# Decode softmax in three visits, values from three groups sooner, conv loads by pairs, and the last additions on one engine

## The chip, the core and the metric

The kernel runs on one core of a Trainium2 chip. The metric is device time in microseconds (us) of one execution; the kernel before is given by the median of three runs. The engines are named as in the profile: PE (TensorE, the matrix engine; PEld its weight loads), DVE (VectorE), ACT (ScalarE), POOL (GpSimd) and SP (SyncE, which here only issues DMAs). Each engine works through its own instructions in order, and semaphores join them.

## What is computed

One layer of a decoder for 512 prompt rows behind 16 learned ones, and 32 rows of eight samples that decode four tokens each over 512 cached positions in pages of 128. With `h` the normalised rows:

```python
q, k, v, ga, cb, cc, ch, gc, ma, mc = split(h @ w_in)        # w_in 2048 x 12288
a = stick_breaking(q, k, v) * silu(ga)                       # 8 heads of 128
c = cb * causal_conv3(cc * ch) * silu(gc)
m = sigmoid(ma + b_ga) * (a @ w_pa) + sigmoid(mc + b_gc) * (c @ w_pc)
y = x + rmsnorm(m @ w_out)

# stick_breaking, in log space:
z = q @ k.T / sqrt(128) + b_h
keep = where(s < t, log_sigmoid(-z), 0)
A = where(s < t, exp(log_sigmoid(z) + sum of keep between s and t), 0)
out = A @ v
```

The samples use the same layer over the cached keys and values in pages that a table names.

## The kernel before, in words

All products stand for fp32 by splitting both sides into a high and a low part (`whi`, `wlo` for weights, `_hi`, `_lo` for rows) and adding three products. So each weight block of 1024x128 is loaded (`raw`, on SP's queue), cast on ACT (`whi`) and subtracted on DVE (`wlo`); five `raw` and three split blocks are kept. The rows lie transposed, features on partitions, 272 queries to a matmul.

The stages, in the time of the profile: the start and the norm, to 60; heads 0 to 3 with their attention, and keys and values of heads 4 to 7 (these go to DRAM), to 390; the gate `ga` and the conv inputs, and then the two sigmoid gates (820 to 1191.8). The last ones are Strassen-Winograd products (`seven`): of two column blocks each, seven products of 24 matmuls instead of eight, with the sums `h11 - h12` and so on prepared in six tiles `t_hi`, `t_lo` of the pool `tt`. Products 3, 5 and 7 read the first, second and third pair of these tiles, the others read `h_hi`, `h_lo`. From 1191.8 to about 1345 come the conv output products with `w_pc`, 16 column blocks of 48 matmuls, and among them the attention of heads 4 to 7 (`head_here`, which reads keys, values and queries back from DRAM); then the products with `w_pa`, then `w_out` by `seven` again with the way back to rows (`rows`), and a tail that scales each row and adds it to `x` (`finish`).

The decoding of the samples runs beside all of this as a generator, `decode_steps`, which a caller advances by `dec_step(n)`. Its steps are: 64 steps of logits (cached keys `kpage` on DVE times queries, `pr`, then summed on ACT into `junk` with an accumulator, or on DVE); then the softmax in two visits, over 1024 columns at once; then the values: cached pages `vpage` on POOL's queue, eight buffers, 80 matmuls of 32x512 each in one of four column strips of PE (`tile_position`), 64 with cached pages and 16 with the new rows (`v_new`), and a copy `ob` and four transposes behind each twenty. `dec_group` is called behind each of 32 gate groups and says how many steps are taken there:

```python
        if n <= 29:
            dec_step(1 if 4 < n <= 20 else 1 + n % 2, "logits")
        elif n == 30:
            dec_step(64, "weights")
        else:
            dec_step(1)
```

Between the gates and the conv products, eight blocks of `c_scr` are loaded into tiles of the pool `g3` (four buffers, made once `tt` is closed), and split into `c_hl`, which takes the place of `h_hi` (tag "A").

The order of the instructions on each engine is fixed when the kernel is built, by a scheduler that places every instruction by its own estimate of times; `keep_in_program_order` (`pin` in the new lines) holds an instruction among its neighbours on its engine. ACT needs a table of functions for each kind: Exp, Ln, Sigmoid; where a function isn't in the loaded one, a load (ACT_TABLE_LOAD) stands in front of it.

Of the kernel before, what the change touches and what calls it, by code (L numbers as in the profile page):

```python
# [59 lines left out]
def hybrid_step_kernel(  # L60
# [341 lines left out]
    def softplus_parts(e, l, r, t, src, bias, neg_bias=None):  # L402

        act.activation(e, src, AF.Abs, bias=bias)
        act.activation(e, e, AF.Exp, scale=-1.0)
        act.activation(l, e, AF.Ln, bias=one_c[:e.shape[0]])
        act.activation(r, src, AF.Relu, bias=bias)
# [114 lines left out]
    def attend(pl, h, khi, klo, vhi, vlo, qr):  # L522
# [18 lines left out]
        def tl(name, g, dt=F32):  # L541
            return pl.tile([P, GW[g]], dt, name=name + str(GW[g]), bufs=1 if g == "A" else 2)
# [62 lines left out]
    def head_now(h):  # L605
# [4 lines left out]
        dec_step(1, "part")  # L610
# [25 lines left out]
    def decode_steps():  # L636
# [50 lines left out]
        with tc.tile_pool(name="dec2", bufs=1, side="right") as d2:  # L687
# [9 lines left out]
            tc.keep_in_program_order(act.preload_act_table_set(LNEXP))  # L697
# [3 lines left out]
            softplus_parts(e[:TS, :BHT], l[:TS, :BHT], rn, t[:TS, :BHT], zn, zero_c[:TS])  # L701
            softplus_parts(e, l, r, t, zf, zero_c)
            mask_new(rn)
# [7 lines left out]
            for pg in reversed(range(NPG)):  # L711
                rp = r[:, pg * BHT:(pg + 1) * BHT]
                pz = z_ps()[:, :BHT]
                pe.matmul(pz, lhsT=neg_u.bitcast(F32), rhs=rp, start=True, stop=False)
                pe.matmul(pz, lhsT=neg_one.bitcast(F32), rhs=S, start=False, stop=True)
                dve.tensor_add(flat(z_all[:, pg]), pz, flat(z_all[:, pg]))
                act.activation(flat(A_all[:, pg]), flat(z_all[:, pg]), AF.Exp)
                if pg > 0:
                    dve.tensor_add(S, S, rp)
# [78 lines left out]
    ttp = tctx.enter_context(tc.tile_pool(name="tt", bufs=1))  # L798
# [468 lines left out]
```

## Time and profile before

| | us |
|---|---|
| median of 3 runs | 1667.27 |
| lowest and highest run | 1665.84, 1668.06 |
| the profiled execution | 1665.04 |
| its span | 1663.5 |
| PE busy in the span | 1604.2 (96%) |
| DVE, ACT, POOL busy | 1254.3, 997.6, 268.3 |
| mean granted clock of PE | 0.985 |

The profile is of one execution. Its span runs from the first to the last recorded event; 1.5 us of the execution lie around it. Busy time is by the profiler's records, and some matmuls may be missing from them. "PEclk" is the granted clock as a share of the full 2.4 GHz; 0.50 is the lower level, 1.2 GHz. A wait is given with what ended it last. "DMA share" is the mean busy share of the 16 DMA engines, and may pass 1.00 a little.

### The profile page before, as it was taken

The page shows a single profiled execution, that of the slowest core. Times are in us where ns is not written, and L with a number is a line of the kernel's source. Part 1 is how long each engine was busy: PE and PEld are TensorE (multiplying, and loading weights), DVE is VectorE, ACT ScalarE, POOL GpSimd, SP SyncE. Part 2 cuts the span into 40 slices and gives each one's busy share as a digit, 9 for nine tenths or more (in the row PEclk, how much of TensorE's full clock was granted, in tenths as well). Part 3 has the DMA queues.
Part 4 walks back from the last instruction along what each step waited for, and adds up shares of the span by engine and source line. Part 5 has one row for each costly group of instructions (what it writes and reads, how often), then busy time and mean ns, then how long its engine had stood idle before and what let it go on. Part 6 is the DMA issues. An engine that isn't in the chain of part 4 may idle for free.

```text
span 1663.5 us, 31665 instructions
## 1 busy us (share of the span) xinstructions
PE 1604.2 (96%) x12174; PEld 1537.3 (92%) x12174; DVE 1254.3 (75%) x1669; ACT 997.6 (60%) x2549; POOL 268.3 (16%) x476
## 2 busy tenths in 40 slices
PE   7999999999999999999999999999989999999995
PEld 6999999999999999999999999878657999999995
DVE  4538888798879898989888888855346667877775
ACT  6247887746765656565667677953356663445552
POOL 0033233222101010000011011031323230000002
PEclk7999999999999999999999999999989999999998
DMA  9265545435544444444455454364866555533335
GB/s 225 77 177 155 155 144 160 143 119 173 177 129 124 130 139 128 133 123 134 134 167 163 145 173 136 103 206 147 266 228 217 160 161 171 157 108 97 94 105 193
DMA packets 306445, 252.72 MB, mean 152 GB/s; under 512 B 11570, under 2 KB 276854, under 8 KB 305190
## 3 DMA queue, kind: packets, MB, share of 16 engines
q1 hardware_dynamic: 276965, 157.44, 33.0%
q0 software_dynamic: 29296, 93.26, 17.4%
q8 instruction: 95, 1.56, 0.4%
q14 instruction: 57, 0.46, 0.1%
q10 hardware_dynamic: 32, 0.01, 0.0%
HBM read 217.95 MB, written 32.71 MB: 151 GB/s over the span
## 4 chain that ended last, share of the span: by engine, by line
PE 65%; issue 10%; DVE 7%; ACT 7%; DMA 3%; POOL 1%; POOLq 0%; DVEq 0%; SPq 0%; ACTq 0%
PE mm L251 22%; PE mm L845 21%; PE o L845 17%; ACT junk L662 2%; DVE pr L656 2%; ACT whi L235 2%; DMA raw<-in_w_in 2%; DVE wlo L236 1%; PE z L591 1%; PE o L601 1%; PE z L537 1%; PE z L845 1%; PE tp L745 1%; DVE xa L1154 0%; DMA kpage<-in_cache_k 0%
## 5 line engine op out<-in xcount | busy, mean ns | idle before, releaser
L235 ACT CAST whi<-raw 128x1024 fp32r<-128x1024 f32 x251 | 262.8, 1049 | 260.6 <-PE o L845 76.2
L236 DVE TENSOR_TENSOR wlo<-raw,whi 128x1024 fp32r<-128x1024 f32 x251 | 306.4, 1221 | 83.2 <-ACT whi L235 62.9
L845 PE MATMUL mm<-h_hi,whi 128*128 128x272 f32 (+1 forms) x1152 | 334.2, 290 | 4.7 <-ACT whi L235 4.6
L845 PE MATMUL mm<-h_lo,whi 128*128 128x272 f32 (+1 forms) x1152 | 332.5, 289 | 0.0
L845 PE MATMUL mm<-h_hi,wlo 128*128 128x272 f32 (+1 forms) x1152 | 332.2, 290 | 0.0
L845 PE MATMUL o<-t_hi,whi 128*128 128x272 f32 (+1 forms) x864 | 253.3, 293 | 7.2 <-DVE c L871 3.1
L845 PE MATMUL o<-t_hi,wlo 128*128 128x272 f32 (+1 forms) x864 | 250.9, 290 | 1.5 <-DVE wlo L236 1.5
L845 PE MATMUL o<-t_lo,whi 128*128 128x272 f32 (+1 forms) x864 | 250.7, 290 | 0.0
L236 DVE TENSOR_TENSOR wlo<-s,whi 128x1024 fp32r<-128x1024 f32 x126 | 154.6, 1227 | 98.4 <-ACT whi L235 98.2
L845 PEld LDWEIGHTS mm<-h_hi,whi 128*128 128x128 f32 x1152 | 217.4, 189 | 9.4 <-ACT whi L235 6.4
L845 PEld LDWEIGHTS mm<-h_lo,whi 128*128 128x128 f32 x1152 | 217.0, 188 | 2.5 <-issue 2.5
L845 PEld LDWEIGHTS mm<-h_hi,wlo 128*128 128x128 f32 x1152 | 216.4, 189 | 2.8 <-issue 2.5
L662 ACT ACTIVATE junk<-pr 128x128 f32<-128x128 f32 x592 | 182.7, 309 | 29.4 <-DVE pr L656 17.2
L235 ACT CAST whi<-s 128x1024 fp32r<-128x1024 f32 x126 | 131.6, 1045 | 100.2 <-PE o L845 31.1
L251 PE MATMUL mm<-h_hi,whi 128*128 128x280 f32 (+1 forms) x640 | 187.2, 293 | 0.0
L251 PE MATMUL mm<-h_hi,wlo 128*128 128x280 f32 (+1 forms) x640 | 187.0, 293 | 0.0
L251 PE MATMUL mm<-h_lo,whi 128*128 128x280 f32 (+1 forms) x640 | 186.7, 292 | 0.0
L845 PEld LDWEIGHTS o<-t_hi,whi 128*128 128x128 f32 x864 | 164.0, 190 | 16.1 <-issue 5.0
L845 PEld LDWEIGHTS o<-t_hi,wlo 128*128 128x128 f32 x864 | 164.1, 190 | 2.4 <-DVE wlo L236 2.4
L845 PEld LDWEIGHTS o<-t_lo,whi 128*128 128x128 f32 x864 | 164.7, 191 | 0.0
L656 DVE TENSOR_TENSOR pr<-kpage,qb 128x1024 f32<-128x1024 f32 x128 | 152.3, 1218 | 8.1 <-DMA qb<-q_scr 3.7
L251 PEld LDWEIGHTS mm<-h_hi,whi 128*128 128x128 f32 x640 | 120.5, 188 | 0.7
(362 smaller groups left out, 3463.8 us busy)
## 6 DMA issues: line engine op xcount, KB each, us to landing
raw<-in_w_in SPq DMA_DIRECT2D x192, 512.0 KB, 4.3
kpage<-in_cache_k POOLq DMA_DIRECT2D x64, 256.0 KB, 3.4
qb<-q_scr POOLq DMA_DIRECT2D x32, 512.0 KB, 5.7
vpage<-in_cache_v POOLq DMA_DIRECT2D x64, 256.0 KB, 5.4
raw<-in_w_out SPq DMA_DIRECT2D x32, 512.0 KB, 4.1
gate_scr<-g POOLq DMA_DIRECT2D x32, 272.0 KB, 3.4
gt<-gate_scr POOLq DMA_DIRECT2D x16, 544.0 KB, 4.0
raw<-in_w_pc SPq DMA_DIRECT2D x16, 512.0 KB, 4.8
```

The costliest lines, as they stand in the source:

```text
L235: act.copy(hi, x)
L236: dve.tensor_sub(lo, x, hi.bitcast(F32))
L251: pe.matmul(o, lhsT=w, rhs=r[:, t0:t1], start=(k == 0 and n == 0), stop=(k == nk - 1 and n == 2))
L537: pe.matmul(zt[:m, c0:c0 + n], lhsT=l[:, s0:s0 + m], rhs=r[:, ts:ts + n], start=(c0 == 0 and i == 0), stop=(i == 2), skip_group_check=True)
L591: pe.matmul(o, lhsT=l, rhs=x, start=False, stop=(i == len(ops) - 1), skip_group_check=True)
L601: pe.matmul(ot[:, ts - NMETA:ts - NMETA + n], lhsT=l[:m, st, :], rhs=x[:m, c0:c0 + n], start=False, stop=(g == GROUPS[-1] and i == 2), ski ...
L656: dve.tensor_mul(pr, kt.unsqueeze(1).broadcast_to([P, 2, 512]), qt))
L662: act.activation(junk, pr[:, t, h * P:(h + 1) * P], AF.Copy, accum_out=z_all[:, pg, b, 4 * hf + h, 2 * i + t:2 * i + t + 1])
L745: pe.matmul(po[32 * j:32 * (j + 1), :], lhsT=lhs, rhs=rhs, start=(pg == 0), stop=(pg == NPG), tile_position=(0, 32 * j), skip_group_check= ...
L845: pe.matmul(o, lhsT=l[:, k, :], rhs=r, start=(start and k == 0 and m == 0), stop=(stop and k == 7 and m == 2), skip_group_check=True)
```

## The change

It has eight parts:

- heads 0 to 3 advance the decoding by six steps each where they did five;
- `dec_group` takes the logits up to group 28 (seven steps are left to it there), the softmax in groups 28, 29 and 30, and two steps of values in each further group;
- the softmax has three visits: pages 2 and 3 with the new rows, pages 0 and 1, and the last Exp over 1024 columns at once, its ACT instructions pinned;
- the table for Exp and Ln is loaded behind the last gate's sigmoid, and no longer in the middle of the `w_out` products;
- `tt` becomes three pools, `tt0` to `tt2`, and each is given back by itself;
- the eight loads of `c_scr` go by two into four tiles, `head_here` gets its inputs from a pool of its own (`headin`), the first of them loaded ahead, and `gt` moves from POOL's queue to SP's;
- in `rows`, the last 32 rows have a PSUM tile of their own, and their product is laid out as 128x512 (`ogr`), so that one addition does them; a matmul with `to4` brings their factor to the 128 partitions;
- in `finish` all additions are on DVE, most of them 1024 wide, none on POOL, and the stores go out on SP's and ACT's queues in turn.

The core of the diff:

```diff
         khi, klo = k_split(np_, k_proj(h))
-        dec_step(1, "part")
+        dec_step(2, "part")
...
-            pn = z_ps()[:TS, :BHT]
-            pe.matmul(pn, lhsT=neg_u.bitcast(F32)[:TS, :TS], rhs=rn, start=True, stop=True)
-            dve.tensor_add(zn, pn, zn)
-            act.activation(zn, zn, AF.Exp)
+            for p0 in (2, 0):
+                pin(act.preload_act_table_set(LNEXP))
+                if p0:
+                    softplus_parts(e[:TS, :BHT], l[:TS, :BHT], rn, t[:TS, :BHT], zn, zero_c[:TS], pin)
+                    mask_new(rn)
+                c = slice(p0 * BHT, (p0 + 2) * BHT)
+                softplus_parts(e[:, c], l[:, c], r[:, c], t[:, c], zf[:, c], zero_c, pin)
+                if p0:
+                    pn = z_ps()[:TS, :BHT]
+                    pe.matmul(pn, lhsT=neg_u.bitcast(F32)[:TS, :TS], rhs=rn, start=True, stop=True)
+                    dve.tensor_add(zn, pn, zn)
+
+                for pg in (p0 + 1, p0):
+                    rp = r[:, pg * BHT:(pg + 1) * BHT]
+                    pz = z_ps()[:, :BHT]
+                    pe.matmul(pz, lhsT=neg_u.bitcast(F32), rhs=rp, start=True, stop=False)
+                    pe.matmul(pz, lhsT=neg_one.bitcast(F32), rhs=S, start=False, stop=True)
+                    dve.tensor_add(flat(z_all[:, pg]), pz, flat(z_all[:, pg]))
+                    if pg > 0:
+                        dve.tensor_add(S, S, rp)
+                yield
+            pin(act.preload_act_table_set(LNEXP))
+            pin(act.activation(zn, zn, AF.Exp))
             mask_new(zn)
-            yield
...
-        if n <= 29:
+        if n <= 27:
             dec_step(1 if 4 < n <= 20 else 1 + n % 2, "logits")
-        elif n == 30:
-            dec_step(64, "weights")
+        elif n == 28:
+            dec_step(64, "logits")
+            dec_step(1)
+        elif n <= 30:
+            dec_step(1)
         else:
-            dec_step(1)
+            dec_step(2)
...
-    ttp = tctx.enter_context(tc.tile_pool(name="tt", bufs=1))
-    t_hi = [ttp.tile([P, 8, HU], F32R, name=f"t_hi{i}") for i in range(3)]
-    t_lo = [ttp.tile([P, 8, HU], F32R, name=f"t_lo{i}") for i in range(3)]
+    t_hi, t_lo = [], []
+    for i in range(3):
+        ttp = tctx.enter_context(tc.tile_pool(name=f"tt{i}", bufs=1))
+        t_hi.append(ttp.tile([P, 8, HU], F32R, name=f"t_hi{i}"))
+        t_lo.append(ttp.tile([P, 8, HU], F32R, name=f"t_lo{i}"))
     h_f, l_f = h_hi.bitcast(F32), h_lo.bitcast(F32)
...
                 act.activation(gs[m][:, by_query(m, half)], b, AF.Sigmoid, bias=gate_bias(j + m, w))
+            if j + 2 * w == KD:
+                tc.keep_in_program_order(act.preload_act_table_set(LNEXP))
             for m in range(2):
                 gate_out(j + m, w, gs[m])
...
+    hl = cctx.enter_context(tc.tile_pool(name="headin", bufs=1))
     cp = cctx.enter_context(tc.tile_pool(name="later", bufs=1))
-    for k in range(8):
-        cr = g3.tile([P, 2, TQ], F32, tag="gt", name="cr")[:, 0, :]
-        nc.sync.dma_start(cr, c_scr[k])
-        split_evac(c_hl[:, k, :], c_hl[:, 8 + k, :], cr, cr)
+    cp2 = cctx.enter_context(tc.tile_pool(name="later2", bufs=1))
+
+    def head_loads(h):
+        kr = hl.tile([P, T], F32, name="kr")
+        nc.sync.dma_start(kr, k_scr[h])
+        qr = hl.tile([P, PQ], F32, name="qr")
+        nc.sync.dma_start(qr, qt_scr[h][:, 0:PQ])
+        vn = hl.tile([P, 5, P], F32, name="vn")
+        nc.sync.dma_start(vn[:, 0:4, :], vn_scr[h][0:512].rearrange("(a p) d -> p a d", p=P))
+        nc.sync.dma_start(vn[0:16, 4, :], vn_scr[h][512:TP])
+        return kr, vn, qr
+
+    loaded = head_loads(NOW)
+    for k in range(0, 8, 2):
+        cr = g3.tile([P, 2, TQ], F32, tag="gt", name="cr")
+        for i in range(2):
+            nc.sync.dma_start(cr[:, i, :], c_scr[k + i])
+            split_evac(c_hl[:, k + i, :], c_hl[:, 8 + k + i, :], cr[:, i, :], cr[:, i, :])
 
     def gated(h, x, sg):
 
...
+        kr, vn, qr = loaded if h == NOW else head_loads(h)
+        ot = attend(cp, h, *k_split(cp, kr), *v_split(cp, vn), qr, cp2)
         gated(h, ot, sg_load(h)[:, 0, 0:PQ])
...
-        pool.dma_start(gt, gate_scr[j][:, 1, :])
+        nc.sync.dma_start(gt, gate_scr[j][:, 1, :])
...
+                pe.transpose(out=pr, in_=tb[:, ROWS[4][0]:ROWS[4][0] + REST], identity=ident)
             for b, i in enumerate(ii):
                 square(i, j, pt[:, b * P:(b + 1) * P], P)
             dve.tensor_mul(og4[:, ii[0]:ii[-1] + 1, cs], pt[:, :n].rearrange("p (i c) -> p i c", c=P),
                            g.unsqueeze(1).broadcast_to([P, len(ii), P]))
             if rest:
-                square(4, j, pt[:REST, n:n + P], REST)
-                dve.tensor_mul(og_rest(cs), pt[:REST, n:n + P], g[:REST])
-
-        def finish(ii, npool):
+                square(4, j, pr, REST)
+                r0, c0 = j // 4 * REST, j % 4 * P
+                dve.tensor_mul(ogr[r0:r0 + REST, c0:c0 + P], pr, g[:REST])
...
+            queues = cycle((nc.sync, act))
             for b, i in enumerate(ii):
-                n = ROWS[i][1]
+                if i == 4:
+                    continue
+                for c0, c1 in zip(cuts[b], cuts[b][1:]):
+                    xc = xs_[i][:, c0:c1]
+                    dve.scalar_tensor_tensor(out=xc, in0=og4[:, i, c0:c1], scalar=rs[:, b:b + 1], in1=xc,
+                                             op0=ALU.mult, op1=ALU.add)
+                    p0, p1, dst = outs[i][0]
+                    next(queues).dma_start(dst[:, c0:c1], xc[p0:p1])
+                for p0, p1, dst in outs[i][1:]:
+                    next(queues).dma_start(dst, xs_[i][p0:p1])
+            if ii[-1] == 4:
+                r4 = t_ps()[:, 0:1]
+                pe.matmul(r4, lhsT=to4.rearrange("p a b -> p (a b)"), rhs=rs[:REST, w - 1:w], start=True, stop=True)
+                r4s = op.tile([P, 1], F32, name="r4s")
+                act.copy(r4s, r4)
+                dve.scalar_tensor_tensor(out=xs_[4], in0=ogr, scalar=r4s, in1=xs_[4], op0=ALU.mult, op1=ALU.add)
+                dst = outs[4][0][2]
                 for c in range(4):
-                    cs = slice(c * CW, (c + 1) * CW)
-                    og = og4[:n, i, cs] if i < 4 else og_rest(cs)
-                    xc, r = xs_[i][:n, cs], rs[:n, b:b + 1]
-                    if c < 4 - npool[b]:
-                        dve.scalar_tensor_tensor(out=xc, in0=og, scalar=r, in1=xc, op0=ALU.mult, op1=ALU.add)
-                    else:
-                        act.activation(og, og, AF.Copy, scale=r)
-                        pool.tensor_add(xc, xc, og)
-                    for p0, p1, dst in outs[i]:
-                        nc.sync.dma_start(dst[:, cs], xc[p0:p1])
+                    next(queues).dma_start(dst[:, c * CW:(c + 1) * CW], xs_[4][c * REST:(c + 1) * REST])
 
...
             product(o, both[m], m_rhs(1, 1), False, True)
             act.copy(cols[m][:, half(1)], o)
             rows(j + m, (2, 3), cols[m], g[:, m], True)
-        finish((2, 3, 4), (1, 1, 2))
+        finish((2, 3, 4), ((0, D // 2, D), (0, D // 2, 3 * CW, D)))
     mctx.close()
 
```

Three places show how the order moves. First, SP's queue at the passage from the gates to the conv products; `cr` are the tiles for `c_scr`, `kr`, `vn`, `qr` the inputs of head 4. Before:

```order
L229 DMA raw<-in_w_pc 128x8x128 x7
L1008 DMA cr<-c_scr 128x544 x4
L229 DMA raw<-in_w_pc 128x8x128
L1008 DMA cr<-c_scr 128x544 x4
L1023 DMA kr<-k_scr 128x560
L1025 DMA vn<-vn_scr 128x4x128
```

After:

```order
L229 DMA raw<-in_w_pc 128x8x128 x4
L1037 DMA cr<-c_scr 128x544 x8
L229 DMA raw<-in_w_pc 128x8x128
L1025 DMA kr<-k_scr 128x560
L1027 DMA qr<-qt_scr 128x512
L1029 DMA vn<-vn_scr 128x4x128
```

The eight loads of `c_scr` now stand together behind four `w_pc` blocks; they stood in two fours behind seven and eight of them.

Second, PE at the same passage: `o` and `t_hi` are of the last gate product, `tp` with `vpage` or `v_new` are value matmuls, `tp` with `ident` the transposes of their result, `mm` with `c_hl` the conv products. Before:

```order
L845 MATMUL o<-t_hi_5007,wlo 128x272
L745 MATMUL tp<-vpage,z_all 32x512 x3
L745 MATMUL tp<-v_new,z_new 32x512 x4
L753 MATMUL tp<-ident,ob 128x128 x4
L745 MATMUL tp<-vpage,z_all 32x512 x5
L251 MATMUL mm<-c_hl,whi 128x272 x4
L251 MATMUL mm<-c_hl,wlo 128x272
```

After, 60 rows into the conv products:

```order
L251 MATMUL mm<-c_hl,wlo 128x272
L251 MATMUL mm<-c_hl,whi 128x272
L752 MATMUL tp<-vpage,z_all 32x512
L251 MATMUL mm<-c_hl,whi 128x272
L251 MATMUL mm<-c_hl,wlo 128x272
L251 MATMUL mm<-c_hl,whi 128x272 x2
L752 MATMUL tp<-vpage,z_all 32x512
```

Twelve value matmuls stood in a heap before the first conv products, with the transposes of the first twenty among them. Now these transposes have gone ahead into the gates, seven value matmuls are left at the head of the conv products (not shown), and the next ten stand one by one among them.

Third, ACT in the group with the longest stretch between two weight casts (`whi`); `junk` sums logits, `g` is a gate's sigmoid, `de` belongs to the softmax. Before:

```order
L235 CAST whi<-s 128x1024
L662 ACTIVATE junk,z_all<-pr 128x128
L990 ACTIVATE g<-c,bg 128x272
L662 ACTIVATE junk,z_all<-pr 128x128 x7
L990 ACTIVATE g<-o,bg 128x272
L662 ACTIVATE junk,z_all<-pr 128x128 x4
L697 ACT_TABLE_LOAD
L990 ACT_TABLE_LOAD
L990 ACTIVATE g<-c,bg 128x272
L404 ACTIVATE de<-z_new,zero_c 32x256
L859 ACTIVATE o<-mm 128x272
L235 CAST whi<-s 128x1024
```

After:

```order
L664 ACTIVATE junk,z_all<-pr 128x128 x6
L1002 ACTIVATE g<-o,bg 128x272
L723 ACT_TABLE_LOAD
L664 ACTIVATE junk,z_all<-pr 128x128 x3
L871 ACTIVATE o<-mm 128x272
L664 ACTIVATE junk,z_all<-pr 128x128
L1002 ACT_TABLE_LOAD
L1002 ACTIVATE g<-c,bg 128x272
L664 ACTIVATE junk,z_all<-pr 128x128 x2
L703 ACT_TABLE_LOAD
L404 ACTIVATE de<-z_new,zero_c 32x256
L235 CAST whi<-s 128x1024
```

A third table load stands in the stretch where there were two, since a sigmoid comes between the two preloads; the number of `junk` is the same.

## Rows read from the trace of the kernel before

**Rows 1.** The page, busy time, share of span and instructions of PE and others:

```profile
PE 1604.2 (96%) x12174; PEld 1537.3 (92%) x12174; DVE 1254.3 (75%) x1669; ACT 997.6 (60%) x2549; POOL 268.3 (16%) x476
```

**Rows 2.** Windows: length, busy PE, PEld, DVE, ACT, POOL, PEclk, DMA share, GB/s.

```profile
1170.00:1180.00 10.00, 10.00 (x75) 7.54 (x74) 2.81 (x3) 3.54 (x5) 3.24 (x6) 1.00 0.75 225
1191.77:1237.45 45.68, 36.22 (x173) 20.45 (x173) 16.40 (x34) 20.58 (x32) 12.89 (x24) 0.89 0.86 290
1200.00:1210.00 10.00, 6.91 (x39) 4.62 (x40) 2.45 (x4) 2.22 (x5) 1.79 (x4) 1.00 1.06 367
1230.62:1237.45 6.83, 6.21 (x27) 5.82 (x28) 3.88 (x12) 6.75 (x11) 1.08 (x2) 0.50 0.41 141
```

**Rows 3.** PE's waits, 1190 to 1235: waiter, releaser: us, times, longest.

```profile
PE mm L251 <- ACT c_hl L423: 4.2, 3, 2.9
PE tp L753 <- ACT ob L750: 2.3, 2, 1.6
PE z L537 <- ACT qhi L423: 1.6, 1, 1.6
```

**Rows 4.** PE's groups, 1191.80 to 1237.40: records | busy us, mean ns | idle before.

```profile
L251 PE MATMUL mm<-c_hl,whi 128*128 128x272 f32 x64 | 17.2, 350 | 4.9 <-ACT c_hl L423 4.2 <-DVE gt L1048 0.6
L745 PE MATMUL tp<-vpage,z_all 128*32 128x512 f32 x38 | 13.2, 627 | 0.6 <-PE tp L753 0.6
L251 PE MATMUL mm<-c_hl,wlo 128*128 128x272 f32 x31 | 9.7, 329 | 0.0
L745 PE MATMUL tp<-v_new,z_new 32*32 32x512 f32 x16 | 2.1, 600 | 0.0
```

**Rows 5.** SP's issues, 1189 to 1206: start, us, queue, line, what.

```profile
1191.87 2.03 SPq L1008 DMA_DIRECT2D cr<-c_scr  x4
...
1198.96 5.88 SPq L1008 DMA_DIRECT2D cr<-c_scr  x4
```

**Rows 6.** Windows of the decode softmax, columns as above.

```profile
1052.00:1080.00 28.00, 23.88 (x160) 22.57 (x159) 21.27 (x29) 27.60 (x46) 3.86 (x4) 0.88 0.33 96
1059.95:1066.78 6.83, 6.43 (x27) 6.11 (x27) 5.24 (x6) 6.78 (x9) 0.00 (x0) 0.50 0.24 76
```

**Rows 7.** PE's waits, 1000 to 1085.

```profile
PE mm L845 <- ACT whi L235: 3.1, 3, 1.7
PE o L845 <- ACT whi L235: 2.3, 1, 2.3
```

**Rows 8.** ACT's groups, 1220 to 1365: one line's table loads.

```profile
L406 ACT ACT_TABLE_LOAD x8 | 10.3, 1283 | 0.1
```

**Rows 9.** PE in time, 1103.5 to 1106: a single value matmul, and the next.

```profile
1104.10 1.05 PE L745 MATMUL tp<-vpage,z_all 128*32 128x512 f32 x2
1105.08 0.39 PE L845 MATMUL o<-t_hi,whi 128*128 128x272 f32 x1
```

**Rows 10.** PE in time, 1170.8 to 1173.2: five value matmuls, two rounds.

```profile
1171.05 1.91 PE L745 MATMUL tp<-vpage,z_all 128*32 128x512 f32 x12
```

**Rows 11.** A window among heads 0 to 3, columns as above.

```profile
220.00:240.00 20.00, 20.00 (x155) 19.71 (x155) 19.13 (x27) 19.27 (x67) 7.38 (x10) 1.00 0.68 200
```

**Rows 12.** PE's waits, 1235 to 1345.

```profile
PE mm L251 <- DVE gt L1048: 0.8, 1, 0.8
PE z L591 <- ACT hi L423: 0.6, 2, 0.4
```

**Rows 13.** The chain that ended last, 1645 to 1664: start, us, what.

```profile
1647.51 0.37 ACT sq L1119 x2
```

**Rows 14.** DVE in time, 1645 to 1664: start, us, line, what.

```profile
1649.50 8.74 DVE L1154 SCALAR_TENSOR_TENSOR xa<-og_a,rs,xa 128x512 f32<-128x512 f32 x7
1658.17 0.73 DVE L1154 SCALAR_TENSOR_TENSOR xa<-ogr,rs,xa 32x512 f32<-32x512 f32 x1
```

**Rows 15.** POOL in time, 1640 to 1664.

```profile
1650.30 3.41 POOL L1157 TENSOR_TENSOR xa<-xa,og_a 128x512 f32<-128x512 f32 x2 [11.52 <-ACT og_a L1156]
```

**Rows 16.** SP's issues, 1654 to 1664: the last stores.

```profile
1654.28 6.93 SPq L1159 DMA_DIRECT2D out<-xa  x12
```

More of the change, by code (lines that the diff above doesn't have):

```diff
@@ L400, in hybrid_step_kernel, with softplus_parts @@
     q_scr = dram.tile([TS, DA], F32, name="q_scr")
[L402 to L407, printed above, removed]
+    def softplus_parts(e, l, r, t, src, bias, pin=lambda ins: ins):
+        pin(act.activation(e, src, AF.Abs, bias=bias))
+        pin(act.activation(e, e, AF.Exp, scale=-1.0))
+        pin(act.activation(l, e, AF.Ln, bias=one_c[:e.shape[0]]))
+        pin(act.activation(r, src, AF.Relu, bias=bias))
         dve.tensor_scalar(out=t, in0=e, scalar1=1.0, scalar2=-1.0, op0=ALU.add, op1=ALU.add)
@@ L520, in v_proj, with attend @@
         return v_split(pl, vn)
-    def attend(pl, h, khi, klo, vhi, vlo, qr):
+    def attend(pl, h, khi, klo, vhi, vlo, qr, pl_a=None):
         qhi = pl.tile([P, T], F32R, name="qhi")
@@ L541, in tl @@
         def tl(name, g, dt=F32):
-            return pl.tile([P, GW[g]], dt, name=name + str(GW[g]), bufs=1 if g == "A" else 2)
+            if g == "A":
+                return (pl_a or pl).tile([P, GW[g]], dt, name=name + "A", bufs=1)
+            return pl.tile([P, GW[g]], dt, name=name, bufs=2)
         def mask(x, g):
@@ L706, in decode_steps @@
-            dve.tensor_add(zn, pn, zn)
-            act.activation(zn, zn, AF.Exp)
-            mask_new(zn)
-            yield
[L711 to L719, printed above, removed]
+            for p0 in (2, 0):
[18 more added lines that the diff above has]
+                yield
@@ L1105, in hybrid_step_kernel @@
     with tc.tile_pool(name="outp", bufs=1) as op:
-        ogr = op.tile([REST, D - CW], F32, name="ogr")
-        def og_rest(cs):
-            return og_a[:REST, 4 * D + cs.start:4 * D + cs.stop] if cs.stop <= CW else \
-                ogr[:, cs.start - CW:cs.stop - CW]
+        ogr = op.tile([P, CW], F32, name="ogr")
+        to4 = op.tile([REST, 4, REST], F32, name="to4")
+        dve.tensor_copy(to4, ident[:REST, :REST].unsqueeze(1).broadcast_to([REST, 4, REST]))
         ssq = og_a[:, 4 * D + CW:4 * D + CW + 5 * KD].rearrange("p (i j) -> p i j", j=KD)
@@ L1128, in rows @@
             if rest:
-                pe.transpose(out=pt[:REST, n:n + P], in_=tb[:, ROWS[4][0]:ROWS[4][0] + REST], identity=ident)
+                pr = t_ps()[:REST, :P]
+                pe.transpose(out=pr, in_=tb[:, ROWS[4][0]:ROWS[4][0] + REST], identity=ident)
             for b, i in enumerate(ii):
@@ L1219, in hybrid_step_kernel @@
         xa = tok.tile([P, 4, D], F32, tag="A", name="xa")
-        xs_ += [xa[:, i, :] for i in range(3)]
+        xs_ += [xa[:, 0, :], xa[:, 1, :], xa[:, 2, :CW]]
         parts = [((0, n, xp[t0:min(t0 + n, PQ), :]),) for t0, n in ROWS]
@@ L1225, in hybrid_step_kernel @@
         outs[3] = ((0, np_, yp[t0:PQ, :]), (np_, P, ys))
-        for i in range(5):
+        for i in range(4):
             load_rows(xs_[i], parts[i])
-        finish((0, 1), (1, 1))
+        for c in range(4):
+            nc.sync.dma_start(xs_[4][c * REST:(c + 1) * REST], parts[4][0][2][:, c * CW:(c + 1) * CW])
+        finish((0, 1), ((0, D // 2, D),) * 2)
         both = []
```

16 lines of the change are left out of this document (2 added, 14 removed).

## The prediction

> **What bounds the kernel now.** I read the busy table first: TensorE (PE) is busy 96% of the span [rows 1]. So the bound is PE's own work, and a change moves the time only where PE waits, where its work grows, or behind its last matmul. I then cut the span into windows and looked for those whose PE time falls short of the window or whose granted clock is below 1.00; third came PE's waits in these windows; fourth the few microseconds behind the last matmul. Three places stand out.
>
> Place A is the passage from the gates to the conv products, 1191.77 to 1237.45. PE is busy 36.2 of 45.7 us, at a mean clock of 0.89, and in the last 6.8 us of it at 0.50, which is the lower of its two levels, 1.2 GHz [rows 2]. It waits for `c_hl` (4.2 us), for the decode output `ob` (2.3) and for the query split (1.6) [rows 3].
>
> Place B is the decode softmax, 1052 to 1080: busy 23.9 of 28.0 us, 6.8 us of it at clock 0.50, while ACT is busy 27.6 of the 28.0 [rows 6]. PE's waits there are for weight casts on ACT, 3.1 and 2.3 us [rows 7].
>
> Place C is the tail. The last seven 128x512 additions and the one of 32 rows run from 1649.50 to 1658.90, and the last store is issued at 1661.21 [rows 14, 16].
>
> **Place A: loads and table.** The window holds 64 + 31 = 95 conv matmuls and 38 + 16 records of value matmuls [rows 4] out of 173 in all [rows 2], so 24 others. A matmul of 272 to 512 columns takes 0.13 us where nothing waits (155 in 20.0 us [rows 11]): 119 x 0.13 = 15.5 us. The value matmuls stand in 11 runs and 14 rounds by the order; a run alone delays the next matmul by about 1.05 us, and each further round by 1.91 - 1.05 = 0.86 [rows 9, 10]. That is 11 x 1.05 + 3 x 0.86 = 14.1 us. Together 29.6, so 16.1 us of the 45.7 are lost: in waits, in the time at half clock behind them, and in matmuls that are issued singly as `c_hl` trickles in.
>
> Before, four of the eight `c_scr` loads are issued at 1191.87 and four more from 1198.96 to 1204.84 [rows 5], since the `g3` buffers lie where all six tiles of `tt` lay, whose last reader is the last product of the gates. After, four tiles of two rows take all eight, and they lie where `tt0` lay, which is read last in the third of seven products. The four products behind it are 96 matmuls, 96 x 0.13 = 12.5 us, so the loads may start some 12 us earlier, and the order puts all eight before the fifth `w_pc` load. The casts to `c_hl` still wait for the last product on `h_hi`, the sixth, one product (3.1 us) before the end. I leave 2.5 us of the 16.1, the query wait of 1.6 and one of about a microsecond for `ob`: -13.6. Bounds: -15.5 when nothing is left, -6 when the loads stay late (rival 2).
>
> In the rest of the conv phase 17 table loads of 1.28 us on ACT go (eight of them in one row [rows 8], nine more at the two lines beside it). ACT has slack there: PE's waits in the whole stretch are 0.8 us for `gt` and 0.6 for the score splits among its largest [rows 12]. I take these two away, -1.4. `gt` now stands on SP's queue among the weight loads: where it waits for a `g3` buffer, the next `raw` waits behind it, and PE with it once the three split weights are used up. A product pair lasts 48 x 0.13 = 6.2 us and needs one load, so I expect none of that; one such block would cost about what the late query cost, 1.6 [rows 3]. Bounds -2 to +2.
>
> **Values.** The order gives 36 runs with 43 rounds before, 46 runs with 50 rounds after, for the same 80 matmuls: batches of five or seven in front of the conv products become singles, each between ordinary matmuls. By the prices above 36 x 1.05 + 7 x 0.86 = 43.8 us, and 46 x 1.05 + 4 x 0.86 = 51.7: +7.9. It lies on the path, since PE is the bound. Bounds: 0 where the runs fall into waits, +10 where a single also meets a late page.
>
> "TensorEngine Tiling (Array Packing)" in the Trainium skill warns, in its section on tiling modes, that a change of mode drains the array. That speaks against singles. The trace agrees in sign only: a run costs 1.05 against 0.86 for a round inside a run [rows 9, 10], so a switch is worth about 0.2 us. Were the drain all that a new run costs, ten more of them would be 2 us in place of 7.9, and the time 1654; by the rows a single also leaves three of four column strips idle, and I keep 7.9.
>
> **Place B: the softmax.** Before, it falls into one group: 28.0 - 160 x 0.13 = 7.2 us lost [rows 6]. After, group 28 finishes the logits (seven steps where four stood) and 28 to 30 take one visit each. The order shows that the loads still alternate with the sigmoids, 12 where 14 were, since Sigmoid isn't pinned. The longest stretch on ACT between two weight casts holds 12 `junk` copies and 3 loads, where it was 12 and 2: 1.3 us longer. Two more stretches of 7 to 8 us (row durations laid on the order) come in the neighbouring groups; of such a stretch PE covers about 6 us, two products of 24 x 0.13 that are split ahead. So 7.2 + 1.3 for the longest and 2.0 + 0.9 for the others: 11.4 against 7.2, +4. Bounds: -7 if no wait is left, +15.7 (rival 1).
>
> **Heads.** Heads 0 to 3 take one decode step more each. In 220 to 240 DVE is busy 19.13 and ACT 19.27 of 20.0, but PE all of it at full clock [rows 11]. I cost it at 0, hidden by the look-ahead of PE's weights; without that cover four steps of about a microsecond, +4.
>
> **Place C: the tail.** Seven additions took 8.74 us, 1.25 each, beside POOL's four (two of them 3.41); the last one, which nothing runs beside, took 0.73 [rows 14, 15]. After, DVE does eight pieces' worth of 512 columns and the rest rows as one 128x512: 9 x 0.73 = 6.6 us from 1649.50, to 1656.1 instead of 1658.9: -2.8. The last square no longer waits behind a multiplication that shares its PSUM tile, -0.4 [rows 13]. SP issues 12 stores in 6.93 us, 0.58 each, and ends 2.3 after the last addition [rows 16]; with two queues the four last stores take 1.2: -1.1. Sum -4.3. The rest rows' scale goes over PE and ACT, about a microsecond, beside 6 us of additions: nothing. Bounds -6 to -2 (the other end if DVE runs at 1.0 a piece).
>
> **Sum.** -13.6 - 1.4 + 7.9 + 4 + 0 - 4.3 = -7.4. The profiled execution took 1665.04, so 1657.6; the median of before is 1667.27, 2.2 above that execution: 1660.
>
> **Rivals.**
> Rival 1, slower: ACT is crowded in three groups instead of one. If PE idles in each of groups 28 to 30 as it did at 1059, its clock falls to 0.50 in each, and each loses the 7.2 us of place B, the longest 1.3 more: 22.9 - 7.2 = +15.7 in place of +4, so 1660 + 11.7 = 1671.7. For it: ACT was busy 27.6 of 28.0. Against: the two new stretches are 2 to 3 us shorter than the old. It decides from waits of about 3 us within one group, which is what they summed to in that place [rows 7]. Chance 0.10.
>
> Rival 2: place A is held by transfers, not by when they are issued. From 1200 to 1210 the queues move 367 GB/s at a share of 1.06, and from 1170 to 1180, where the loads would now go, they are already at 0.75 [rows 2]. Then the earlier loads only push the pages, and of the 16.1 us about 10 stay: 1660 + 7.5 = 1667.5, no change. Against: 12 us are gained for 2.2 MB, which take 6 us at 367 GB/s. "DMA: Bandwidth & Descriptors" in the Trainium skill, section on issuing engines, says that all queues share the same 16 DMA engines, so that a move from POOL's queue to SP's brings only issue time. By that rule an earlier issue saves issue time alone while the 16 are full, which is this rival; the rows show them full for at least 10 of the 45.7 us, which is why it has a chance of 0.15. Chance 0.15.
>
> Rival 3, better: the earlier values fall into PE's waits for weight casts in groups 31 and 32 and cost nothing, and the three visits leave no more lost than the one did: 1660 - 7.9 = 1652.1, less if the +4 goes too: 1648. Chance 0.20.
>
> Forecast, 0.55: 1655 to 1666.
>
> **How the numbers follow.** This measurement can tell about 0.2%, 3.3 us, from no change: faster is below 1663.9, slower above 1670.6. Of the forecast's 0.55 some 0.45 lies below 1663.9, the rest is within; rival 3 gives 0.20 of faster; rival 2 splits 0.03, 0.11 and 0.01; rival 1 gives 0.08 of slower and 0.02 of the same. So faster 0.68, same 0.23, slower 0.09. For 8 in 10 the range reaches down to half of rival 3 and up past rival 2: 1650 to 1669.
>
> **What would show it.** Right: all eight `c_scr` loads issued before the last product of the gates ends; no time at half clock between the gates and the first conv products; PE busy all but 2 or 3 us of that stretch; singles of value matmuls at 1.05 us each; the last addition at about 1656. Wrong, step by step: `c_hl` still named in PE's waits (place A); a clock of 0.50 in more than one of groups 28 to 30 (softmax); value runs with a gap of PE before them (late pages); `raw` late behind `gt` on SP; DVE's last additions over 1 us without POOL. The whole is wrong if the passage still loses 10 us, or if the weight casts make PE wait more than 12 us in the three groups.

## The result and the profile after

The changed kernel takes 1675.09 us, the median of 22 runs (1673.75 to 1680.58), the kernel before 1670.91 (22 runs, 1665.84 to 1676.03): a ratio of 1.0028, 95% interval 1.0019 to 1.0036. It is slower by about 0.3%, where 0.4% faster was forecast (1660 from 1667.27), and it lies outside the range of 1650 to 1669.

The trace of before that the prediction rests on is of an execution of 1665.04 us, and with 22 runs that is below the fastest of them. So a second trace of the kernel before was taken, of 1671.22 us; it stands in the table as "before, second". A stage is read from the last matmul that reads the gates' rows (`h`, `t`), `c_hl` and `a_hl`.

| us | gates end | conv products | w_pa products | from there to the end | span |
|---|---|---|---|---|---|
| before | 1191.8 | 169.2 | 101.4 | 201.1 | 1663.5 |
| before, second | 1195.7 | 169.8 | 103.1 | 201.1 | 1669.6 |
| after | 1202.5 | 154.1 | 118.1 | 198.5 | 1673.2 |

Against the second trace the gates end 6.8 us later, the conv products take 15.7 less, the `w_pa` products 15.0 more, and the tail 2.6 less. The page of the changed kernel, its span, busy time and granted clock in 40 slices:

```profile
span 1673.2 us, 31637 instructions
PE 1618.0 (97%) x12176; PEld 1542.7 (92%) x12176; DVE 1248.7 (75%) x1670; ACT 966.7 (58%) x2526; POOL 257.3 (15%) x454
PEclk7999999999999999999999999999999988999998
```

The dip has moved: before it lay at the passage, at half clock [rows 2]; now the clock is full there, and slices 33 and 34, in which the `w_pa` products begin, are below. The windows say the same; the columns are those of [rows 2], the first window is the passage, the second the first 26.6 us of the `w_pa` products, the third the whole stretch at half clock:

```profile
1202.50:1248.20 45.70, 45.70 (x277) 30.93 (x277) 21.74 (x41) 19.12 (x32) 16.68 (x31) 1.00 0.91 307
1356.60:1383.20 26.60, 18.78 (x97) 15.26 (x96) 8.73 (x17) 6.83 (x12) 3.88 (x12) 0.72 0.33 111
1368.40:1388.90 20.50, 15.74 (x54) 12.53 (x55) 9.42 (x19) 6.80 (x12) 2.22 (x8) 0.50 0.18 56
```

At the passage PE is busy all the time with 277 matmuls, where it got 173 done in the same 45.7 us before [rows 2]. In the first 26.6 us of the `w_pa` products it gets 97 done, at a mean clock of 0.72. In the second trace of before the same stretch is nearly full, at full clock:

```profile
1365.50:1392.00 26.50, 25.18 (x189) 23.92 (x188) 16.11 (x31) 12.30 (x19) 3.94 (x10) 1.00 0.45 140
```

PE's waits in the stage, as in [rows 3], and PE in time at the places where they end:

```profile
PE z L593 <- ACT hi L423: 4.1, 1, 4.1
PE o L603 <- ACT hi L423: 1.7, 1, 1.7
PE mm L251 <- ACT a_hl L423: 1.4, 1, 1.4
PE z L593 <- ACT l L423: 0.6, 1, 0.6
```

```profile
1369.43 0.60 PE L593 MATMUL z<-hi,neg_u 128*128 128x272 f32 x1 [4.09 <-ACT hi L423]
...
1376.46 0.70 PE L603 MATMUL o<-hi,vhi 128*128 128x400 f32 x1 [1.70 <-ACT hi L423]
...
1383.18 1.05 PE L251 MATMUL mm<-a_hl,whi 128*128 128x272 f32 x3 [1.43 <-ACT a_hl L423]
```

L593 and L603 are the score sums and the values of an attention; `a_hl` is its result. This is head 7, the last of the four that are computed among the conv products. Its last half now stands among the first 63 of the `w_pa` matmuls; its last score sums and all its values come behind these 63 with no other matmul between them, so that each step waits for the one before. POOL in time shows where a part of its lateness is from (each row: start, length, what; in brackets the idle time before and what ended it):

```profile
1354.88 0.54 POOL L1089 DMA_DIRECT2D gt<-gate_scr  x1
1359.22 0.54 POOL L1089 DMA_DIRECT2D gt<-gate_scr  x1 [3.80 <-DMA gate_scr<-gt]
1359.77 0.45 POOL L550 TENSOR_SCALAR_AFFINE_SELECT r<-r 128x128 f32<-128x128 f32 x2
1360.18 0.57 POOL L1072 DMA_DIRECT2D gate_scr<-gt  x1
1367.70 0.54 POOL L1089 DMA_DIRECT2D gt<-gate_scr  x1 [6.95 <-issue]
1368.24 0.56 POOL L550 TENSOR_SCALAR_AFFINE_SELECT r<-r 128x128 f32<-128x128 f32 x2
```

Two masks of head 7's scores (L550) stand behind loads of `gt` for the `w_pa` products (L1089). Before these loads POOL is idle for 3.8 and 6.95 us, until a store of a conv block has landed: the store issued at 1354.33 lands at 1358.94, the one issued at 1360.18 at 1367.18.

The other places. The eight `c_scr` loads are issued together, 13.6 us before the gates end, where they took from 1191.87 to 1204.84, behind the end of the gates [rows 5]:

```profile
1188.88 3.66 SPq L1037 DMA_DIRECT2D cr<-c_scr  x8
```

At the softmax PE waits about as long as it did [rows 7], now for two casts and once for a mask on POOL:

```profile
PE o L857 <- ACT whi L235: 3.8, 1, 3.8
PE z L711 <- POOL dS L686: 1.8, 1, 1.8
PE mm L857 <- ACT whi L235: 0.4, 1, 0.4
```

In the tail, DVE, then SP and ACT as issuers of stores, in time; the additions take 5.7 us in all, where they took 9.4 [rows 14]:

```profile
1661.29 5.00 DVE L1176 SCALAR_TENSOR_TENSOR xa<-og_a,rs,xa 128x1024 f32<-128x1024 f32 x5
1666.21 0.75 DVE L1187 SCALAR_TENSOR_TENSOR xa<-ogr,r4s,xa 128x512 f32<-128x512 f32 x1
```

```profile
1662.61 4.05 SPq L1179 DMA_DIRECT2D out<-xa  x3
1666.99 1.74 SPq L1190 DMA_DIRECT2D out<-xa  x2
```

```profile
1666.99 1.86 ACTq L1190 DMA_DIRECT2D out<-xa  x2
```

One more reading, of the order alone. Head 7's first scores stand behind 592 of the 768 conv matmuls in the kernel before, and behind 683 in the changed one; its last score sums stand behind 5 of the `w_pa` matmuls before, and behind 63 after. This was to be seen before the run.

### The profile page after: what moved, and what is told of

Same layout as the page of the kernel before. It is cut to its first block, busy times and chain, and to the rows that moved or that the text cites. A ratio compares the mean times of both kernels' runs of the same rounds, so it can differ in the third digit from the quotient of the medians.

```text
span 1673.2 us, 31637 instructions
## 1 busy us (share of the span) xinstructions
PE 1618.0 (97%) x12176; PEld 1542.7 (92%) x12176; DVE 1248.7 (75%) x1670; ACT 966.7 (58%) x2526; POOL 257.3 (15%) x454
## 3 DMA queue, kind: packets, MB, share of 16 engines
q0 software_dynamic: 28016, 88.80, 16.1%
## 5 line engine op out<-in xcount | busy, mean ns | idle before, releaser
L236 DVE TENSOR_TENSOR wlo<-raw,whi 128x1024 fp32r<-128x1024 f32 x251 | 306.2, 1220 | 85.8 <-ACT whi L235 70.9
L857 PE MATMUL o<-t_hi,wlo 128*128 128x272 f32 (+1 forms) x864 | 252.0, 292 | 1.3 <-DVE wlo L236 1.3
L658 DVE TENSOR_TENSOR pr<-kpage,qb 128x1024 f32<-128x1024 f32 x128 | 152.4, 1218 | 13.5 <-DMA qb<-q_scr 7.1
```

The source lines that it names most:

```text
L236: dve.tensor_sub(lo, x, hi.bitcast(F32))
L658: dve.tensor_mul(pr, kt.unsqueeze(1).broadcast_to([P, 2, 512]), qt))
L857: pe.matmul(o, lhsT=l[:, k, :], rhs=r, start=(start and k == 0 and m == 0), stop=(stop and k == 7 and m == 2), skip_group_check=True)
```

## The experiments

Ratios are against the kernel before on the same chip, with 95% intervals; "faster" and "slower" in us go by them. "Below the changed kernel" is a difference of medians from different batches of runs, in which the kernel before itself has medians of 1670.0 to 1672.7, so it is good to about 3 us. Theory H: the `w_pa` stage is long because head 7's attention has become last. The rivals stand in each expectation.

**The kernel before once more** (no edit).

> The kernel before once more, unchanged, for a second trace: its runs spread from 1665.8 to 1676.0 us, and the trace that the prediction was made from is of an execution of 1665.0, at the fast end. Theory H (the loss lies in the w_pa stage, where head 7's attention has become last): the w_pa stage lasts about 101 us here too, and the passage from the gates to the conv products again loses about 16 us; what differs is a DMA landing later somewhere. Rival: the fast trace was the exception, and a usual execution also stalls in the w_pa stage by 5 us or more.

1671.22 us. The conv stage takes 169.8 us and the `w_pa` stage 103.1, so the usual execution has no stall there of 5 us or more: the rival falls. It is 3.9 us later at the end of the gates than the fast one and 1.7 longer in the `w_pa` stage; what makes it so was not found.

**gt for the w_pa products on SP's queue.**

```diff
-            pool.dma_start(gt, gate_scr[j])
+            nc.sync.dma_start(gt, gate_scr[j])
```

> The changed kernel with the 16 loads of gt for the w_pa products on SP's queue instead of POOL's. In the trace of after, two masks of head 7's scores on POOL stand behind such loads, which wait for stores of the last conv blocks: 3.5 and 5.3 us. Theory P (the head-of-line wait on POOL makes head 7 late): 8 us faster than the changed kernel (1667), the w_pa stage 110 us in place of 118. Rival (head 7 is late because its scores start late): 0 to 3 us faster. A loss would say that SP's weight loads now wait behind gt.

1669.88 us (0.9987, 0.9969 to 1.0005), 5.2 below the changed kernel (6.9 by the ratios). The `w_pa` stage is 108.6 us in place of 118.1, the conv stage 3.6 longer. So the waits on POOL's queue are a part, about 9 us of the stage, but not all, and the masks' place is not what put head 7 there.

**Heads 5 to 7 called earlier.**

```diff
-    HERE = {0: 4, 3: 5, 6: 6, 9: 7}
+    HERE = {0: 4, 1: 5, 4: 6, 7: 7}
...
-            k = j // 3
+            k = HERE[j] - NOW
```

> The changed kernel with heads 5, 6 and 7 called at columns 1, 4 and 7 of the conv products instead of 3, 6 and 9. By the order head 7's first scores then stand behind 620 conv matmuls instead of 683 of the 768. Theory H: 63 matmuls of 0.13 us are 8 us, and the w_pa stage shortens by about that: 1667. Rival (the w_pa stage is slow for another reason, such as its loads): no change from the changed kernel, 1675.

1665.09 us (0.9953, 0.9935 to 0.9972), 10 below the changed kernel (12.5 by the ratios). In the kernel that ran head 7's first scores stand behind 613 conv matmuls, its values still behind 63 of the `w_pa` matmuls. The `w_pa` stage is 104.9 us, 13.2 shorter, for 3.1 more in the conv stage. Theory H holds, the rival falls.

**Without head 7's attention.**

```diff
-        ot = attend(cp, h, *k_split(cp, kr), *v_split(cp, vn), qr, cp2)
+        ot = qr if h == 7 else attend(cp, h, *k_split(cp, kr), *v_split(cp, vn), qr, cp2)
```

> The changed kernel without the attention of head 7 (its query rows stand in for the result, so that part of the output is not computed); nothing else differs. Theory H: the stall of the w_pa stage goes, some 15 us, and with it PE's own work for that head, about 9 us: 1651. Rival (the loss in the w_pa stage isn't head 7's): only the 9 us of work go: 1666.

1654.7 us (0.9894, 0.9873 to 0.9915), 20 below the changed kernel (22 by the ratios). The `w_pa` stage is 96.6 us, which is what its 768 matmuls take at 0.126. In the traces the conv and `w_pa` stages are 20.2 us shorter together: 11.7 of them are idle time and time at half clock, 8.5 the head's own work, near the expectation's 9 (the account below).

**The passage alone** (the kernel before with three `tt` pools, `c_scr` by pairs, head inputs ahead; gt stays on POOL).

```diff
-    for k in range(8):
-        cr = g3.tile([P, 2, TQ], F32, tag="gt", name="cr")[:, 0, :]
...
+    for k in range(0, 8, 2):
+        cr = g3.tile([P, 2, TQ], F32, tag="gt", name="cr")
```

> The kernel before with the parts of the change at the passage alone: three pools for tt, the eight c_scr loads by pairs, the head inputs from a pool of their own, loaded ahead; gt stays on POOL's queue, softmax, values and tail as before. Theory H (what the passage gains comes back where head 7's attention ends in the w_pa stage): the stage of the conv products is 12 to 16 us shorter than before, the w_pa stage 10 to 15 longer, the time within 3 us of before: 1670. Rival (the forecast: the gain of the passage stands): 14 us faster, 1657.

1663.24 us (0.9956, 0.9938 to 0.9974): 7.4 us faster than before. The conv stage is 156.3 us, 13.5 less than in the second trace; the `w_pa` stage 108.6, 5.5 more. Between the two expectations: the saving at the place itself is the forecast's, and two fifths of it come back one stage later, with head 7 in PE's waits there, though gt stays on POOL's queue. In this kernel too its first scores stand late, behind 668 conv matmuls, and its values behind 63 of the `w_pa` matmuls:

```profile
PE o L603 <- ACT hi L423: 1.7, 1, 1.7
PE mm L251 <- ACT a_hl L423: 1.4, 1, 1.4
```

**Softmax and values alone** (three visits, two steps of values a group, six steps in the heads; the rest as before).

```diff
         khi, klo = k_split(np_, k_proj(h))
-        dec_step(1, "part")
+        dec_step(2, "part")
...
         else:
-            dec_step(1)
+            dec_step(2)
```

> The kernel before with the softmax in three visits, the earlier values and the sixth step in the heads alone. The gates are to end about 7 us later (6.8 between the two traces), from more value matmuls there and the stall at the softmax. Theory H: the conv products have as many value matmuls fewer, but head 7's attention sets their end, so little comes back: 3 to 7 us slower than before. Rival (the forecast's prices, 7.9 for the values and 4 for the softmax, all on the path): 12 us slower, 1683. Second rival: the values' time is only moved: no change.

1679.29 us (1.0053, 1.0033 to 1.0074): 8.9 us slower, between theory H and the first rival. The gates end 5.8 us later than in the second trace, the conv stage is 6.0 shorter, and the `w_pa` stage 6.6 longer: what leaves the conv products comes back behind them here as well. So the second rival (time only moved) would hold for gates and conv products, and the loss that is left has the size of what stands in the `w_pa` stage. Head 7 stands late here as well, behind 668 and 63, without any other part of the change.

**The tail alone.**

```diff
-        finish((2, 3, 4), (1, 1, 2))
+        finish((2, 3, 4), ((0, D // 2, D), (0, D // 2, 3 * CW, D)))
```

> The kernel before with the new tail alone (rows, finish and the layout of the last 32 rows). The forecast: 4.3 us faster. By the two traces the stretch from the last w_pa product to the end is 2.6 us shorter: 1668 to 1669. Rival: the additions on one engine lose what the stores gain: no change.

1666.3 us (0.9975, 0.9962 to 0.9988): 4.2 us faster, as forecast; in the trace the stretch behind the `w_pa` products is 3.1 us shorter.

**Both mendings together** (heads earlier, and gt of the `w_pa` products on SP).

> The changed kernel with both mendings: heads 5, 6 and 7 called at columns 1, 4 and 7, and the gt loads of the w_pa products on SP's queue. Theory H with P: head 7 is early enough that its masks no longer meet the loads, so the second mending adds little to the first: 1662 to 1665. Rival: the two add up, 5 us more: 1660.

1667.24 us (0.9976, 0.9960 to 0.9992), above both expectations and not below the first mending alone. The `w_pa` stage is 103.6 us, 1.3 less than with the earlier heads alone. They don't add up, but not for the reason expected: with the earlier heads alone the two masks still stand behind loads of `gt`, after 2.6 and 3.0 us of idle POOL (the second is shown), and taking the loads away gains the stage little:

```profile
1359.56 0.54 POOL L1089 DMA_DIRECT2D gt<-gate_scr  x1 [2.99 <-DMA gate_scr<-gt]
1360.11 0.57 POOL L550 TENSOR_SCALAR_AFFINE_SELECT r<-r 128x128 f32<-128x128 f32 x2
```

**gt of the conv products back on POOL's queue** (one line of the change undone).

```diff
-        nc.sync.dma_start(gt, gate_scr[j][:, 1, :])
+        pool.dma_start(gt, gate_scr[j][:, 1, :])
```

> The changed kernel with one part undone: gt of the conv products stays on POOL's queue, as before the change. In the order this alone brings head 7's first scores back to where they stood before, behind 592 conv matmuls instead of 683, and its last score sums from 63 w_pa matmuls to 5. Theory G (the place of head 7 in the order, moved by gt on SP's queue, is the cause): the w_pa stage is 102 us again instead of 118, the stage of the conv products near 156, the whole 1662. Rival (head 7 is late since the conv products end sooner, wherever gt is loaded): the w_pa stage stays over 110 us, 1670 to 1675.

1664.5 us (0.9964, 0.9951 to 0.9977): 10.6 below the changed kernel, by one line. The `w_pa` stage is 101.3 us, as in the kernel before, the conv stage 159.9, 5.8 longer than in the changed kernel. Theory G holds for this pair. The first window of the `w_pa` products, columns as above, is full, at full clock:

```profile
1361.80:1388.40 26.60, 26.57 (x203) 25.66 (x203) 17.94 (x35) 11.01 (x18) 3.98 (x10) 1.00 0.49 148
```

SP's queue itself is not what holds head 7 back. The head's keys (`kr`) are issued 11 us later in the changed kernel, but in both kernels as soon as the last reader of their buffer, DVE's `klo` of head 6, is done, and ACT first reads them 30 us and more after that. DVE, SP and ACT in time, first with gt on POOL:

```profile
1268.43 0.74 DVE L424 TENSOR_TENSOR klo<-kr,khi 128x560 fp32r<-128x560 f32 x1 [3.16 <-ACT khi L423]
1269.20 0.34 SPq L1025 DMA_DIRECT2D kr<-k_scr  x1
...
1307.29 0.65 ACT L423 CAST khi<-kr 128x560 fp32r<-128x560 f32 x1
```

and in the changed kernel:

```profile
1279.56 0.72 DVE L424 TENSOR_TENSOR klo<-kr,khi 128x560 fp32r<-128x560 f32 x1
1280.68 0.36 SPq L1025 DMA_DIRECT2D kr<-k_scr  x1
...
1313.48 0.64 ACT L423 CAST khi<-kr 128x560 fp32r<-128x560 f32 x1
```

So head 6's split is 11 us later already, by the order on the engines, and the loads for head 7 follow it. Why this one line changes the scheduler's order so is not shown. Head 7's values end at 1372 and 1382, 10 us apart.

**All but softmax and values.**

> The changed kernel with the softmax, the values and the heads' decode steps as before; passage, gt on SP, table and tail changed. By the order head 7 stands as late as in the changed kernel (683, 63). Theory G: the w_pa stage is long, 113 to 118 us, though the gates end 7 us sooner: about 1668. Rival (the earlier values make the w_pa stage long): the w_pa stage is near 105 and the time near 1659.

1659.94 us (0.9939, 0.9920 to 0.9958), with the next one the fastest that computes the whole output. The `w_pa` stage is 115.9 us, as theory G says, but the conv stage only 147.1, so that the time is the rival's: 15 below the changed kernel. Head 7 is late and stalls PE as in the changed kernel; what is saved stands in front of it, in the gates (8.4 us) and the conv products (7.0). In this kernel the two stages take 263.0 us together, with gt back on POOL 261.2, with the passage alone 264.9; 272.2 in the changed kernel and 272.9 in the second trace of before.

**Without softmax and values, gt on POOL, heads earlier.**

> What the runs so far point to: passage, table and tail of the change, gt on POOL's queue, softmax and values as before, heads 5, 6 and 7 called at columns 1, 4 and 7. In the order head 7's last products then stand before the last 55 conv matmuls. Theory H or G: gates to 1193, conv products 156 to 160, w_pa 97 to 99, the rest 198: 1651 in the trace, a median of about 1654, 1.0% below before. Rival (the heads' waits now stand in the conv products): the conv products take 165 us or more, 1660.

1660.8 us (0.9936, 0.9921 to 0.9951). The `w_pa` stage is 96.6 us, with no head 7 in it at all, but the conv stage 167.9: the rival. The stall has gone into the conv products, and the sum, 264.5, is no better than that of the run above.

**The same with softmax and values.**

> The same with the softmax and values of the change: the changed kernel with gt on POOL's queue and the earlier heads. Against the run before it, it prices softmax and values by themselves where head 7 isn't the end. By the traces the gates end 7 us later and the conv products have eight value matmuls less: 2 us slower than it, 1656; by the forecast's prices 12 us slower, 1666; by the run of softmax and values alone 9 us, 1663.

1663.47 us (0.9944, 0.9925 to 0.9964), 2.7 slower than the run before it, with intervals that overlap; the gates end 8.3 us later and the two stages behind them take 262.1 us, 2.4 less. That is not 12 and not 9. But it is no clean price: head 7's values stand behind 63 of the `w_pa` matmuls here and before the last 55 conv matmuls in the run before it.

## Why the prediction was wrong

The step that failed is the sum itself: "-13.6 - 1.4 + 7.9 + 4 + 0 - 4.3 = -7.4". It adds what each place saves, and asks of none of them what ends next. No term and no rival of it stands for the `w_pa` stage, which took 15.0 us more. Of the 15 us that the conv products were to lose (-13.6 and -1.4), conv and `w_pa` products together lost 0.7, from 272.9 to 272.2.

- **Place A.** "I leave 2.5 us of the 16.1 [...]: -13.6" is right at its place. The loads come before the end of the gates, PE is full at the passage, and with the passage alone the conv stage is 13.5 us shorter. But 5.5 of them come back in the `w_pa` stage, and in the whole change 15.0 of the 15.7. The attention of heads 4 to 7 is a chain: from the values of one head to those of the next it is 32 to 39 us in the trace of before, 33 to 36 in that of after. From the end of the gates to the end of head 7's values it is 181.7 us in the second trace of before and 179.3 after, so the chain gained little of the 15.7 us that the conv products gained, and more of it was left over for the `w_pa` stage. With gt back on POOL it is 170.1.
- **The -1.4.** Of its two waits, PE's for `gt` stayed (2.0 us in the conv stage behind the passage, as in the second trace of before), and those for the splits of the scores moved into the `w_pa` stage.
- **gt on SP's queue.** "I expect none of that", with bounds of -2 to +2. It was priced as a wait of PE for weights. What it did was to put head 7 91 matmuls later in the order, and undoing it alone gives 10.6 us, far outside its bounds. It has that price only beside the earlier values: head 7 stands late with the passage alone too, gt on POOL, and without softmax and values gt on SP costs about 1 us, with an uncertainty of some 3 (an estimate: the ratios of passage alone and tail alone multiply to 0.9931, all but softmax has 0.9939).
- **Values.** +7.9 for all of them together. Measured from the records (from the matmul before a run to the one behind it, less the 0.126 of an ordinary one): in the gates 18 runs that cost 23.0 us became 25 runs of 29.6, which is 6.6 of the 6.8 by which the gates are later; in the conv products 29.6 us (second trace of before) became 26.0. So +3.0 over both. The forecast left out that the heaps before had waits in them (4.8 us in the second trace). Where they have few, the earlier values cost more than forecast: in all but softmax 31 runs cost 40.1 us, in the changed kernel 46 runs 55.6 (51.7 by the forecast's prices), which is 15.5 us; the medians of the two kernels differ by 15.
- **Softmax.** +4. PE's waits from 1000 to 1085 are 6.0 us, as they were 5.9 (5.4 of them in [rows 7]; 7.3 in the second trace); the three visits cost nothing here. Rival 1, with a drop of the clock in each of three groups, did not come: there is one, of 6.8 us from 1040.7.
- **Heads 0 to 3.** 0, and it is 0: at the 65th weight cast on ACT, about 450 us, the two later traces are 0.5 us apart.
- **Tail.** -4.3, measured -4.2 alone by the times, -2.6 to -3.1 by the traces. Its parts were not as said: the additions end 3.7 us sooner after their start (5.7 for 9.4; 2.8 was forecast), and behind the last store, whose issue ends at 1668.85 on ACT's queue, 4.35 us are left to the end of the span, where it was 2.3 on SP's [rows 16].
- **The base.** 2.2 us lay between the profiled execution and the median of three runs; with 22 runs it is 5.9. From that base the same sum gives 1663.5, still on the faster side.
- **Rival 2**, that transfers hold the passage, is wrong: the DMA share there is 0.91 and PE is never idle. **Rival 3** has no support: the 25 runs in the gates cost 29.6 us, 1.18 each.

Why of two kernels with head 7 equally late one is 15 us faster, an account of the two stages shows. Idle is the stage less PE's busy time; the loss at half clock is half of PE's busy time in stretches at 0.50 (an estimate); the value matmuls are what their runs cost among the conv products, without idle time; the rest is what is left of the two stages, and it lies between 226 and 230 us in all thirteen traces in which head 7 is computed.

| us | conv + w_pa | idle | lost at half clock | value matmuls | rest |
|---|---|---|---|---|---|
| before, second | 272.9 | 12.4 | 6.3 | 25.5 | 228.7 |
| after | 272.2 | 9.8 | 7.9 | 26.0 | 228.5 |
| after, gt on POOL | 261.2 | 6.8 | 2.6 | 22.5 | 229.3 |
| all but softmax | 263.0 | 10.8 | 6.5 | 17.1 | 228.6 |
| passage alone | 264.9 | 12.5 | 7.7 | 17.8 | 226.9 |
| softmax and values alone | 273.5 | 19.2 | 11.1 | 13.6 | 229.6 |
| without head 7 | 252.0 | 2.9 | 3.1 | 26.0 | 220.0 |

Busy time and clock of the two stages, columns as above, are for the changed kernel, the one with gt on POOL, and all but softmax:

```profile
1202.50:1356.60 154.10, 152.13 (x1016) 123.87 (x1016) 93.61 (x179) 75.52 (x131) 40.80 (x72) 1.00 0.61 193
1356.60:1474.70 118.10, 110.28 (x803) 106.76 (x802) 82.24 (x168) 41.00 (x71) 10.78 (x25) 0.91 0.46 141
...
1201.90:1361.80 159.90, 153.16 (x1021) 126.59 (x1022) 98.11 (x188) 78.25 (x135) 51.69 (x93) 0.98 0.61 194
1361.80:1463.10 101.30, 101.27 (x797) 100.36 (x797) 77.85 (x158) 39.01 (x67) 9.28 (x20) 1.00 0.50 152
...
1194.10:1341.20 147.10, 143.13 (x1035) 123.25 (x1036) 93.86 (x183) 76.47 (x132) 38.92 (x76) 1.00 0.69 219
1341.20:1457.10 115.90, 109.06 (x804) 105.53 (x803) 82.35 (x169) 41.07 (x71) 10.76 (x25) 0.93 0.46 144
```

The change only moved the stall: idle and half clock are 18.7 us before and 17.7 after, at another place. With gt on POOL they are 9.4. In all but softmax they are 17.3, as in the changed kernel, and there the values are 8.9 us cheaper. So two things met in the changed kernel, a stall from a late head 7 and values that run as singles, and undoing either one was enough to be faster than before. In softmax and values alone the values are cheap and the stall is larger instead, 30.3. Open is why the order comes out so: head 7 stands behind 592 conv matmuls in the kernel before and in the changed one with gt on POOL, behind 668 in passage alone and in softmax and values alone, and behind 683 in the changed kernel and in all but softmax.

## What to carry to other kernels

A stall that is removed is gained only if nothing else in its stage was using it: before adding up savings, look for the chain that runs beside the stage (here an attention per 35 us) and ask where its last piece falls when the stage is shorter. The order of the instructions tells without a run where the stall will come: count how many matmuls of a stage stand in front of each side chain, before and after. It does not tell the price: all but softmax has the same two counts as the changed kernel, 683 and 63, and is 15 us faster. A load is to be priced by who stands behind it on its queue, above all where it waits for a store to land, as for the masks on POOL here; and where a scheduler fixes the order, a moved load also by the new order, on every engine.

## What the runs showed of the hardware

PE's clock fell to half, 1.2 GHz, at 1368.40, in a stall of 4.09 us that ended at 1369.43, and stayed there for 20.5 us with two more stalls of 1.70 and 1.43 in them. PE was busy 15.74 us of that, with 54 matmuls; the kernel with gt on POOL did 203 at full clock in 26.6 us. So 7.8 us of idle PE in the `w_pa` stage came with about as much again, 7.9, lost at half clock.

The 16 stores of conv blocks in the changed kernel took from 2.3 to 7.0 us until they landed (median 2.7), the slowest the one issued at 1360.18. Two masks on POOL's queue, behind a load that waited for it, started only when the load had gone out, 6.95 us after the instruction in front of it. And a run of value matmuls cost about as much singly as in a heap: in the changed kernel's conv stage 21 runs of 32 matmuls cost 26.0 us, in all but softmax 13 runs of 46 cost 18.9.
